# Hybrid encoder trunk on one core: SSD decay masks on GpSimd, fp32 state products, and split weights kept in DRAM

## Chip, cores and metric

The kernel runs on 1 core of one Trainium2 chip. The metric is the device time of one execution in microseconds (us), lower is better. The median of runs stands for a kernel.

## The reference, cut

One layer of a trunk over 2048 frames of a new stream (the prompt) and 8 running streams of 16 frames (the sample), all fp32, model width 1024:

```python
h = W_out [ gMLP heads (u * (W_s v + b)) || Mamba-2 SSD heads ] (x W_in)
x = LayerNorm(ALPHA * x + h)
x = LayerNorm(ALPHA * x + relu(x W1)^2 W2)
```

The part that the change touches is the SSD scan in the mixer, by chunks of 128 positions, 16 heads of 64 in two groups that share B and C:

```python
acum = cumsum(dt * a)                                  # within a chunk
decay = exp(where(causal, acum[i] - acum[j], -inf))
cb = einsum('bcign,bcjgn->bcijg', C, B)
y_diag = einsum('bcijg,bcijgr,bcjgr,bcjgrp->bcigrp', cb, decay, dt, x)
st = einsum('bcjgn,bcjgr,bcjgrp->bcgrpn', B, exp(acum[-1] - acum) * dt, x)
# over chunks: h = exp(acum[-1]) * h + st
y_off = einsum('bcign,bcgrpn,bcigr->bcigrp', C, h_start, exp(acum))
```

and the projection `x W_in` (1024 x 4624) ahead of it, whose weights the change keeps in another form.

## The kernel before

The 2176 rows are 17 chunks of 128; chunk 0 holds the sample. The mixer (`mixer_heads`) goes over three blocks of 6, 6 and 5 chunks. In each block it goes over 18 units, each a tile of 256 columns of `W_in`, in the order z0, x4, x5, x0, x1, z1, x2, x3, z2, z3, u0 to u3, v0 to v3. A unit multiplies the block's rows by its weights in a split form: each fp32 operand becomes a high and a low part of the type float32r (`split`: a cast on ScalarE at L55 gives the high part, a subtraction on VectorE at L56 the low part), and three products (high high, high low, low high; `PASSES`) are added up in PSUM. Units x and u run as `fl_matmul` (L217, 384 or 256 moving columns), units z and v as `tl_matmul` (L225, 256 columns). For every unit of every block, `load_w` reads the weights in two halves of 512 KB into a staging pool of three buffers and splits them into one of two buffers `w`.

Results of the units go through DRAM. After z1 and after z3 the tasks `ssd(b, j, g)` of the block's chunks j for the two groups g are put in a list, after v3 the tasks `gmlp`; `run(1)` emits one task behind each unit, so a block's last tasks run under the next block's units, and the last ones under the output projection. The program is then put in order by the compiler's scheduler, so that a task's instructions stand between the matmuls of the units. Each engine runs its own list in order. All loads and stores are issued from SP, in order.

A task `ssd` loads `xs`, `bt` (B, positions on partitions), `bc` (B and C transposed), `e` (the cumulative sums `at` of 8 heads, broadcast over partitions, 512 KB) and `z`. TensorE forms `pc` = C B^T (L419); VectorE multiplies it by the triangle `tri` into `cbm` (L421). For 4 of 8 heads (`NACT`) ScalarE forms the clipped difference of cumulative sums with Relu (L425), for the other 4 VectorE does (L427); two exponentials of 512 columns follow (L429, L431). VectorE multiplies the 1024 columns of `e` by `cbm` (L432); TensorE takes the eight products `yd` with `xdt` (L439). The chunk's state `st` is B times `xwt`, and `yo` is C times the state before it; both are three passes over split operands (`product`, L395), for which `bt`, `xwt`, `bc` and the state are split each time (`sm`, `xw_hi`, `xw_lo`, `h_hi`, `h_lo`; the wide ones come from the pool `fp` of 8 buffers). For chunk 0 there is a loop over 8 streams instead, with a plain fp32 `yo` (L469), `st` from split operands (L471), and loads `h` of the streams' states. There are 34 tasks: 2 of chunk 0, and 32 others, of which 30 have a `yo`. VectorE and GpSimd then combine the parts, and a gated norm goes to DRAM (L504).

After the mixer come the output projection (L679) and the feed-forward network (L876, L1064), which the change leaves as they are.

Of the kernel before, what the change touches and what calls it, by code (L numbers as in the profile page):

```python
# [14 lines left out]
P = 128  # L15
# [11 lines left out]
EPS = 1e-5  # L27
BLOCKS = [(0, 6), (6, 6), (12, 5)]
PASSES = ((0, 0), (0, 1), (1, 0))
NACT = 4  # L30
KORDER = [(q, i, k) for q in range(2) for i in range(3) for k in range(4 * q, 4 * q + 4)]


# [57 lines left out]
def mixer_heads(ctx, tc, right, psA, A, O, dr, small, sp, ident, select, rsqrt, split, yg_d, ys_d):  # L91
# [15 lines left out]

    order = ["z0", "x4", "x5", "x0", "x1", "z1", "x2", "x3", "z2", "z3", "u0", "u1", "u2", "u3", "v0", "v1", "v2", "v3"]

    def load_w(u):  # L110
        w = wp.tile([P, 2, KD, 272], F32R, name="w", tag="w")
        for q in range(2):
            load_w_half(w, u, q)
        return w

    def load_w_half(w, u, q):
        n = 272 if u == "z0" else 256
# [23 lines left out]
    for j in range(1, BLOCKS[0][1]):  # L141
        for q in range(2):
            load_x_half(j, q)

    def const(name, src, shape):
        t = cl.tile(shape, F32, name=name)
# [177 lines left out]
    def decays(b):  # L324
        c0, n = BLOCKS[b]
        s = state[b]
        N = n * NH
        tmp = lambda nm: small.tile([P, 6 * NH], F32, name=nm, tag="dtmp", bufs=4)[:, :N]
        xr = s["dt"][:, :n].rearrange("p c h -> p (c h)")
        na = tmp("na")  # L330
        nc.vector.tensor_scalar(na, xr, -1.0, None, op0=ALU.mult)
        nc.vector.tensor_tensor(na, na, xr, op=ALU.min)
        u = tmp("u")
        nc.scalar.activation(u, na, AF.Exp)
        q = tmp("q")
        nc.vector.tensor_scalar(q, u, 2.0, None, op0=ALU.add)
        nc.vector.reciprocal(q, q)
        nc.vector.tensor_mul(u, u, q)
        nc.vector.tensor_mul(q, u, u)
        p = tmp("p")  # L340
        nc.vector.tensor_scalar(p, q, 2.0 / 15, 2.0 / 13, op0=ALU.mult, op1=ALU.add)
        for k in (11, 9, 7, 5, 3, 1):
            nc.vector.tensor_mul(p, p, q)
            nc.vector.tensor_scalar(p, p, 2.0 / k, None, op0=ALU.add)
        nc.vector.tensor_mul(p, p, u)
        dt = s["dt"].rearrange("p c h -> p (c h)")[:, :N]
        nc.vector.scalar_tensor_tensor(dt, xr, 0.0, p, op0=ALU.max, op1=ALU.add)
        da = s["da"]
        dav = da[:, :N]
        nc.vector.tensor_mul(da[:, :N].rearrange("p (c h) -> p c h", h=NH), s["dt"][:, :n],  # L350
                             av.unsqueeze(1).to_broadcast([P, n, NH]))
        d0 = NH if c0 == 0 else 0
        pa = psB.tile([P, 512], F32, name="pa", tag="b")
        for m, m8, o in ((tri, tri8, 0), (gt, gt8, 128), (ones, None, 256)):
            if d0 and m8 is not None:
                nc.tensor.matmul(pa[:, o:o + d0], m8, da[:, :d0], start=True, stop=True)
            lo = d0 if m8 is not None else 0
            nc.tensor.matmul(pa[:, o + lo:o + N], m, da[:, lo:N], start=True, stop=True)
        nc.vector.tensor_copy(s["acum"][:, :N], pa[:, :N])
        nc.scalar.activation(s["ea"][:, :N], pa[:, :N], AF.Exp)  # L360
        nc.scalar.activation(s["dw"][:, :N], pa[:, 128:128 + N], AF.Exp)
        nc.scalar.activation(s["bd"][:, :N], pa[:, 256:256 + N], AF.Exp)
        nc.vector.tensor_mul(s["dw"][:, :N], s["dw"][:, :N], dt)
        pt = psB.tile([P, 512], F32, name="pta", tag="b")
        nc.tensor.matmul(pt[:N, :P], da[:, :N], tri, start=True, stop=True)
        at = small.tile([P, 2, P], F32, name="at", tag="at", bufs=1)
        nc.vector.tensor_copy(at[:N, 0], pt[:N, :P])
        nc.sync.dma_start(s["at"][d0:N], at[d0:N, 0])
        if d0:
            p8 = psB.tile([P, 512], F32, name="p8", tag="b")  # L370
            nc.tensor.matmul(p8[:d0, :P], da[:, :d0], tri8, start=True, stop=True)
            nc.vector.tensor_copy(at[:d0, 1], p8[:d0, :P])
            nc.sync.dma_start(s["at"][:d0], at[:d0, 1])

            dm = small.tile([P, NS, NH], F32, name="dm", tag="dm", bufs=1)
            nc.vector.tensor_mul(dm, ind.unsqueeze(2).to_broadcast([P, NS, NH]),
                                 da[:, :NH].unsqueeze(1).to_broadcast([P, NS, NH]))
            pd = psB.tile([P, 512], F32, name="pd", tag="b")
            nc.tensor.matmul(pd[:, :P], ones, dm.rearrange("p s h -> p (s h)"), start=True, stop=True)
            bd8 = cl.tile([P, NS, NH], F32, name="bd8")  # L380
            nc.scalar.activation(bd8.rearrange("p s h -> p (s h)"), pd[:, :P], AF.Exp)
            s["bd8"] = bd8
# [7 lines left out]
        split(*t, src)  # L390
        return t

    def product(ps, a, b, start=True, stop=True):
        for i, (p, q) in enumerate(PASSES):
            nc.tensor.matmul(ps, a[p], b[q], start=start and i == 0, stop=stop and i == 2)  # L395

    heads = lambda a: a.rearrange("p (h d) -> p h d", h=8)

    def ssd(b, j, g):
# [17 lines left out]
        nc.sync.dma_start(z, s["z"][j, :, g * 512:(g + 1) * 512])  # L417
        pc = psB.tile([P, 512], F32, name="pc", tag="b")
        nc.tensor.matmul(pc[:, :P], bc[:, 0], bc[:, 1], start=True, stop=True)  # L419
        cbm = bp.tile([P, P], F32, name="cbm", tag="cbm")  # L420
        nc.vector.tensor_mul(cbm, pc[:, :P], tri8 if dec else tri)  # L421
        for h in range(8):
            i = j * NH + 8 * g + h
            if h < NACT:
                nc.scalar.activation(e[:, h], e[:, h], AF.Relu, bias=s["acum"][:, i:i + 1], scale=-1.0)  # L425
            else:
                nc.vector.tensor_scalar(e[:, h], e[:, h], s["acum"][:, i:i + 1], 0.0, op0=ALU.subtract, op1=ALU.min)  # L427
        if NACT:
            nc.scalar.activation(e[:, :NACT], e[:, :NACT], AF.Exp, scale=-1.0)  # L429
        if NACT < 8:  # L430
            nc.scalar.activation(e[:, NACT:], e[:, NACT:], AF.Exp)  # L431
        nc.vector.tensor_mul(e, e, cbm.unsqueeze(1).to_broadcast([P, 8, P]))  # L432
        xdt = bp.tile([P, 512], F32, name="xdt", tag="xd", bufs=3)
        nc.gpsimd.tensor_mul(heads(xdt), heads(xs), s["dt"][:, j, 8 * g:8 * g + 8].unsqueeze(2).to_broadcast([P, 8, HD]))
        xwt = bp.tile([P, 512], F32, name="xwt", tag="xd", bufs=3)
# [2 lines left out]
        for h in range(8):  # L438
            nc.tensor.matmul(yd[:, h * HD:(h + 1) * HD], e[:, h], xdt[:, h * HD:(h + 1) * HD], start=True, stop=True)  # L439
        yo = None  # L440
        sm = bp.tile([P, 4, P], F32R, name="sm", tag="sm", bufs=1)
        if dec:
            yo = psB.tile([P, 512], F32, name="yo", tag="b")

# [29 lines left out]
                nc.sync.dma_start(O["ssm_sample"][r][:, g * 512:(g + 1) * 512], h0)  # L474
        else:
            st = psB.tile([P, 512], F32, name="st", tag="b")
            split(sm[:, 0], sm[:, 1], bt)
            product(st, (sm[:, 0], sm[:, 1]), wide(xwt, "xw"))
            hn = bp.tile([P, 512], F32, name="hn", tag=f"hn{g}")
            if first:  # L480
                nc.vector.tensor_copy(hn, st)
            else:
                yo = psB.tile([P, 512], F32, name="yo", tag="b")
                split(sm[:, 2], sm[:, 3], bc[:, 1])
                product(yo, (sm[:, 2], sm[:, 3]), wide(hst[g], "h"))
                nc.gpsimd.tensor_mul(heads(hn), heads(hst[g]), col("bd"))
                nc.vector.tensor_add(hn, hn, st)
            hst[g] = hn
# [73 lines left out]
    for i, (b, u) in enumerate(units):  # L562
        c0, n = BLOCKS[b]
        if u == "z0":
            N = n * P
            s = state[b] = {
                "u": dr.tile([P, 8, N], F32, name=f"u{b}"), "v": dr.tile([n, P, D], F32, name=f"v{b}"),
                "z": dr.tile([n, P, D], F32, name=f"z{b}"), "xs": dr.tile([n, P, D + 256], F32, name=f"xs{b}"),
                "bc": dr.tile([P, 2, 2, N], F32, name=f"bc{b}"), "at": dr.tile([n * NH, P], F32, name=f"at{b}"),
                "dt": cl.tile([P, 6, NH], F32, name=f"dt{b}", tag="dt", bufs=2),  # L570
                "vst": cp.tile([P, 6, 4, 6], F32, name=f"vst{b}", tag="vst", bufs=2),
            }
            for k in ("da", "acum", "ea", "dw", "bd"):
                s[k] = cl.tile([P, 6 * NH], F32, name=f"{k}{b}", tag=k, bufs=1 if k == "da" else 2)
        if i + 1 < len(units):
            nxt[i + 1] = load_w(units[i + 1][1])
        w = nxt.pop(i)
        {"x": unit_x, "z": unit_z, "v": unit_v, "u": unit_u}[u[0]](b, w, int(u[1]))
        if u == "v3" and b + 1 < len(BLOCKS):
            load_x(BLOCKS[b + 1][0], range(BLOCKS[b + 1][1]))  # L580
        if u == "z0":
            decays(b)
        if (b, u) == (0, "x5"):
            gmlp_constants()
        if u == "z1":
            tasks += [(ssd, b, j, 0) for j in range(n)]
        if u == "z3":
            tasks += [(ssd, b, j, 1) for j in range(n)]
        if u == "v3":
            tasks += [(gmlp, b, j) for j in range(n)]  # L590
            if b == len(BLOCKS) - 1:
                break
        run(1)
# [556 lines left out]
```

## Time and profile before

| | us |
|---|---|
| median of 3 runs | 2850.16 |
| lowest and highest run | 2849.03, 2855.03 |
| profiled execution, its own time | 2852.59 |
| span of its trace | 2850.6 |
| TensorE busy in the span | 2759.4 |
| VectorE busy in the span | 1989.4 |
| GpSimd busy in the span | 386.9 |

The profiled execution's own time is 2.0 us over the span of its trace, which begins and ends with the program's own instructions. Busy time of TensorE has matmuls overlapped. Granted clock 1.00 is TensorE's full speed.

### The profile page before, as it was taken

What the parts mean: (1) busy time and instruction counts of PE and PEld (TensorE: products, weight loads), DVE (VectorE), ACT (ScalarE), POOL (GpSimd) and SP (SyncE); (2) the same over time, 40 slices, a digit from 0 to 9 for tenths busy, and PEclk for the clock granted to TensorE, in tenths of its full rate; (3) what the DMA queues carried; (4) which work ended last, traced back from release to release, by engine and by line L of the source; (5) the groups of instructions that cost most, each with busy time, mean ns of one, the idle gap of its engine ahead of it and who ended that gap; (6) DMA issues with size and microseconds to landing.
All of it is one profiled execution on the core that took longest, in us unless ns stands there. A gap on an engine that the chain in (4) does not pass through costs nothing.

```text
span 2850.6 us, 42737 instructions
## 1 busy us (share of the span) xinstructions
PE 2759.4 (97%) x15876; PEld 2546.1 (89%) x15876; DVE 1989.4 (70%) x3218; ACT 1202.5 (42%) x2152; POOL 386.9 (14%) x509
## 2 busy tenths in 40 slices
PE   9999999999999998999998999999999999999998
PEld 8998999999999997887878999999999888888886
DVE  6687878778788777756558777776776344544887
ACT  5445434444444442110115555555665333323343
POOL 1223313323234212100100000000000000000022
PEclk9999999999999999999999999999999999999999
DMA  5465576555565548988569999986877455545764
GB/s 195 137 199 184 183 221 189 163 163 173 186 208 168 182 150 281 286 263 276 174 199 366 317 347 367 348 303 241 284 239 234 154 175 175 177 147 182 261 212 168
DMA packets 420800, 632.49 MB, mean 222 GB/s; under 512 B 74592, under 2 KB 309488, under 8 KB 414448
## 3 DMA queue, kind: packets, MB, share of 16 engines
q1 hardware_dynamic: 420592, 629.77, 67.3%
q8 instruction: 124, 2.03, 0.3%
q14 instruction: 84, 0.69, 0.1%
HBM read 436.16 MB, written 193.51 MB: 221 GB/s over the span
## 4 chain that ended last, share of the span: by engine, by line
PE 65%; DMA 16%; DVE 12%; issue 3%; ACT 2%; POOL 1%; SPq 1%; DVEq 0%; ACTq 0%; POOLq 0%
PE pf L876 22%; PE pf L1064 21%; PE psfl L217 7%; PE pstl L225 6%; PE po L679 4%; DMA e<-at 2%; DMA w1p<-in_w_ff 2%; DMA w1s<-w1p 2%; DVE w L56 1%; PE pf L1029 1%; DVE acc L294 1%; PE yd L439 1%; DMA v<-v 1%; DMA xs<-xs 1%; DMA xv<-xsum 1%
## 5 line engine op out<-in xcount | busy, mean ns | idle before, releaser
L876 PE MATMUL pf<-xt,w 128*128 128x384 f32 (+1 forms) x4032 | 672.0, 329 | 22.0 <-ACT w L55 10.7
L876 PEld LDWEIGHTS pf<-xt,w 128*128 128x128 f32 x4032 | 668.9, 189 | 25.3 <-ACT w L55 11.5
L1064 PE MATMUL pf<-w,ht 128*128 128x512 f32 x2688 | 618.0, 389 | 0.7 <-ACT ht L55 0.7
L1064 PEld LDWEIGHTS pf<-w,ht 128*128 128x128 f32 x2688 | 504.5, 188 | 105.6 <-ACT ht L55 1.1
L217 PE MATMUL psfl<-xw,w 128*128 128x384 f32 (+1 forms) x2880 | 499.6, 331 | 0.0
L217 PEld LDWEIGHTS psfl<-xw,w 128*128 128x128 f32 x2880 | 480.8, 190 | 8.1 <-issue 5.6
L225 PE MATMUL pstl<-w,xw 128*128 128x256 f32 (+1 forms) x3264 | 400.3, 283 | 6.9 <-ACT w L55 6.9
L225 PEld LDWEIGHTS pstl<-w,xw 128*128 128x128 f32 x3264 | 395.0, 189 | 10.2 <-ACT w L55 6.9
L679 PE MATMUL po<-wout,mx 128*128 128x512 f32 x1632 | 379.4, 394 | 10.5 <-ACT mx L55 6.2
L679 PEld LDWEIGHTS po<-wout,mx 128*128 128x128 f32 x1632 | 309.2, 190 | 77.5 <-ACT mx L55 6.8
L56 DVE TENSOR_TENSOR ht<-hr,ht 128x1536 fp32r<-128x1536 f32 (+1 forms) x84 | 132.4, 1576 | 185.2 <-ACT ht L55 182.6
L55 ACT CAST ht<-hr 128x1536 fp32r<-128x1536 f32 (+1 forms) x84 | 112.3, 1337 | 216.1 <-PE pf L1064 194.5
L76 POOL TENSOR_SCALAR frs<-fmv 128x1 f32<-128x1 f32 x17 | 8.9, 525 | 1301.3 <-DVE fmv L983 1300.7
L55 ACT CAST w<-w2r 128x512 fp32r<-128x512 f32 x192 | 110.7, 618 | 135.2 <-PE pf L1064 92.2
L56 DVE TENSOR_TENSOR w<-w2r,w 128x512 fp32r<-128x512 f32 x192 | 124.5, 684 | 61.2 <-ACT w L55 60.9
L55 ACT CAST w<-w1s 128x512 fp32r<-128x512 f32 x192 | 118.6, 619 | 83.3 <-PE pf L876 77.3
L56 DVE TENSOR_TENSOR w<-ws,w 128x1024 fp32r<-128x1024 f32 (+1 forms) x108 | 148.4, 1401 | 5.2 <-ACT w L55 5.1
L56 DVE TENSOR_TENSOR w<-w1s,w 128x512 fp32r<-128x512 f32 x192 | 131.8, 688 | 22.6 <-ACT w L55 18.1
L294 DVE SCALAR_TENSOR_TENSOR acc<-raw,cw,acc 128x640 f32<-128x640 f32 (+1 forms) x108 | 104.1, 964 | 13.4 <-ACT acc L288 12.6
L55 ACT CAST w<-ws 128x1024 fp32r<-128x1024 f32 (+1 forms) x108 | 108.2, 1050 | 7.2 <-DMA ws<-in_w_in 6.0
L55 ACT CAST mx<-mxs 128x512 fp32r<-128x512 f32 x34 | 20.1, 620 | 164.8 <-DMA mxs<-yg 106.2
L56 DVE TENSOR_TENSOR w<-w1r,w 128x512 fp32r<-128x512 f32 x96 | 66.0, 688 | 33.1 <-ACT w L55 31.1
(227 smaller groups left out, 3135.7 us busy)
## 6 DMA issues: line engine op xcount, KB each, us to landing
ws<-in_w_in SPq DMA_DIRECT2D x102, 512.0 KB, 5.2
w1s<-w1s SPq DMA_DIRECT2D x48, 1024.0 KB, 7.6
hr<-hv SPq DMA_DIRECT2D x56, 768.0 KB, 5.3
w1r<-in_w_ff SPq DMA_DIRECT2D x48, 512.0 KB, 7.8
hv<-hs SPq DMA_DIRECT2D x32, 768.0 KB, 5.9
w2r<-w2s SPq DMA_DIRECT2D x80, 256.0 KB, 4.3
e<-at SPq DMA_DIRECT2D x34, 512.0 KB, 6.9
x<-x SPq DMA_DIRECT2D x33, 512.0 KB, 5.7
```

The lines of the kernel that those rows point to most:

```text
L55: nc.scalar.copy(hi, src)
L56: nc.vector.tensor_sub(lo, src, hi.bitcast(F32))
L76: nc.gpsimd.tensor_scalar(out, var, scale, eps, op0=ALU.mult, op1=ALU.add)
L217: nc.tensor.matmul(ps[:, :n], w[:, a, k, f * P:(f + 1) * P], xw[:, b, k, o:o + n], start=(q, i, k) == KORDER[0], stop=(q, i, k) == KORDER[-1])
L225: nc.tensor.matmul(ps[:, :n], xw[:, a, k, j * P:(j + 1) * P], w[:, b, k, :n], start=(q, i, k) == KORDER[0], stop=(q, i, k) == KORDER[-1])
L294: nc.vector.scalar_tensor_tensor(aa, raw[:, k:k + npr], cw[:, ft, k:k + 1], aa, op0=ALU.mult, op1=ALU.add)
L439: nc.tensor.matmul(yd[:, h * HD:(h + 1) * HD], e[:, h], xdt[:, h * HD:(h + 1) * HD], start=True, stop=True)
L679: nc.tensor.matmul(acc[c][d], m[c][k // 4][:, a, k % 4], W[q][:, w, i, d * 512:(d + 1) * 512], start=k == 0 and (a, w) == (0, 0), stop=k = ...
L876: nc.tensor.matmul(o, W[i][:, u, k], X[i][:, v, k, :n], start=q + k == 0 and not more, stop=q == 2 and k == 3, skip_group_check=True)
L1029: nc.tensor.matmul(ps[d], h[:, u, k, f], w[d][:, v], start=k + f + q == 0, stop=(k, f, q) == (n - 1, 1, 2))
L1064: nc.tensor.matmul(acc[l], h[:, u, m, j * P:(j + 1) * P], w[m][:, v], start=kg + q + m == 0, stop=(kg, q, m) == (3, 2, 3))
```

## The change

Four things change, all inside the mixer.

- **Decays.** `cbm` and the clipped differences go. GpSimd writes -1e30 over the entries of `e` above the diagonal (`select`, an affine select over 128x1024; for chunk 0 two more to keep streams apart). ScalarE takes the exponential of each head's 128 columns with the negated cumulative sum as bias (8 instructions). VectorE multiplies `e` by `pc` straight from PSUM.
- **State products.** `st` and `yo` of chunks 1 to 16 are one plain fp32 matmul each, on `bt`, `xwt`, `bc` and the state as they are. Their splits go. Chunk 0 keeps its own.
- **Weight parts.** In block 0 each unit's split weights `w` are written to DRAM, 2 MB (`keep_parts`). In blocks 1 and 2 `load_w` reads these 2 MB straight into `w`; the loads of the raw halves and the splits go.
- `acum` is stored negated (`nacum`).

```diff
+    def load_w(b, u):
+
         w = wp.tile([P, 2, KD, 272], F32R, name="w", tag="w")
+        n = 272 if u == "z0" else 256
+        if b > 0:
+            nc.sync.dma_start(w[:, :, :, :n].bitcast(F32), parts[u])
+            return w
         for q in range(2):
             load_w_half(w, u, q)
+        keep_parts(u, w)
         return w
+
+    def keep_parts(u, w):
+        n = 272 if u == "z0" else 256
+        parts[u] = dr.tile([P, 2, KD, n], F32, name=f"w_{u}")
+        nc.sync.dma_start(parts[u], w[:, :, :, :n].bitcast(F32))
...
-        nc.vector.tensor_copy(s["acum"][:, :N], pa[:, :N])
+        nc.vector.tensor_scalar(s["nacum"][:, :N], pa[:, :N], -1.0, None, op0=ALU.mult)
...
-        cbm = bp.tile([P, P], F32, name="cbm", tag="cbm")
-        nc.vector.tensor_mul(cbm, pc[:, :P], tri8 if dec else tri)
+
+        select(e, [[0, 8], [1, P]], 0, -1, fill=NEVER)
+        if dec:
+            e4 = e.rearrange("p h (s t) -> p h s t", s=NS)
+            select(e4, [[0, 8], [-DS, NS], [0, DS]], 0, 1, fill=NEVER)
+            select(e4, [[0, 8], [DS, NS], [0, DS]], DS - 1, -1, fill=NEVER)
         for h in range(8):
             i = j * NH + 8 * g + h
-            if h < NACT:
-                nc.scalar.activation(e[:, h], e[:, h], AF.Relu, bias=s["acum"][:, i:i + 1], scale=-1.0)
-            else:
-                nc.vector.tensor_scalar(e[:, h], e[:, h], s["acum"][:, i:i + 1], 0.0, op0=ALU.subtract, op1=ALU.min)
-        if NACT:
-            nc.scalar.activation(e[:, :NACT], e[:, :NACT], AF.Exp, scale=-1.0)
-        if NACT < 8:
-            nc.scalar.activation(e[:, NACT:], e[:, NACT:], AF.Exp)
-        nc.vector.tensor_mul(e, e, cbm.unsqueeze(1).to_broadcast([P, 8, P]))
+            nc.scalar.activation(e[:, h], e[:, h], AF.Exp, bias=s["nacum"][:, i:i + 1])
+        nc.vector.tensor_mul(e, e, pc[:, :P].unsqueeze(1).to_broadcast([P, 8, P]))
...
-            split(sm[:, 0], sm[:, 1], bt)
-            product(st, (sm[:, 0], sm[:, 1]), wide(xwt, "xw"))
+            nc.tensor.matmul(st, bt, xwt, start=True, stop=True)
...
-                split(sm[:, 2], sm[:, 3], bc[:, 1])
-                product(yo, (sm[:, 2], sm[:, 3]), wide(hst[g], "h"))
+                nc.tensor.matmul(yo, bc[:, 1], hst[g], start=True, stop=True)
```

## Rows read from the trace of the kernel before

**Rows 1.** The page, part 1: busy us (share of the span) xinstructions.

```profile
PE 2759.4 (97%) x15876; PEld 2546.1 (89%) x15876; DVE 1989.4 (70%) x3218; ACT 1202.5 (42%) x2152; POOL 386.9 (14%) x509
```

**Rows 2.** Windows: busy us (x) of PE, PEld, DVE, ACT, POOL; clock, DMA share, GB/s.

```profile
0.00:387.00 387.00, 371.35 (x2468) 355.09 (x2469) 298.14 (x543) 189.74 (x394) 98.80 (x182) 1.00 0.58 182
387.00:598.00 211.00, 199.62 (x1357) 196.15 (x1357) 163.67 (x279) 88.44 (x179) 62.73 (x73) 0.98 0.60 182
598.00:761.00 163.00, 162.92 (x1162) 160.65 (x1161) 132.87 (x243) 80.52 (x182) 48.29 (x49) 1.00 0.53 170
...
870.00:1021.00 151.00, 144.42 (x983) 140.06 (x982) 114.57 (x199) 72.64 (x168) 56.19 (x55) 0.94 0.57 177
...
1085.00:1140.00 55.00, 44.40 (x207) 35.30 (x206) 42.78 (x80) 15.89 (x22) 16.28 (x16) 0.94 0.98 317
```

**Rows 3.** Waits of PE, 387:1085: who <- by whom: total us, times, longest.

```profile
PE yd L439 <- DVE e L432: 10.6, 6, 3.6
PE sg L533 <- DVE v L522: 6.4, 2, 3.5
```

**Rows 4.** Waits of PE, 0:387.

```profile
PE yo L469 <- DMA h<-in_state_ssm: 4.1, 3, 2.0
```

**Rows 5.** The chain that ended last, 0:600: start us, us, what.

```profile
100.14 16.92 PE pstl L225 x144
...
290.39 0.86 PE yo L469 x2
...
585.32 0.70 PE yo L395 x3
```

**Rows 6.** Timeline, 944:953: start us, us, instruction, idle before it.

```profile
946.99 1.42 DVE L56 TENSOR_TENSOR h_lo<-hn,h_hi 128x512 fp32r<-128x512 f32 x1
947.82 1.49 POOL L436 TENSOR_TENSOR xwt<-xs,dw 128x512 f32<-128x512 f32 x1
...
948.67 1.73 DVE L432 TENSOR_TENSOR e<-e,cbm 128x1024 f32<-128x1024 f32 x1
...
950.54 2.80 PE L439 MATMUL yd<-xdt,e 128*128 128x64 f32 x16 [3.00 <-DVE e L432]
```

**Rows 7.** Groups by line, whole span: busy us, mean ns of one, idle before.

```profile
L56 DVE TENSOR_TENSOR w<-ws,w 128x1024 fp32r<-128x1024 f32 x102 | 140.4, 1403 | 4.0 <-ACT w L55 3.9
...
L425 ACT ACTIVATE e<-e,acum 128x128 f32<-128x128 f32 x136 | 43.9, 391 | 72.1 <-DMA e<-at 72.0
...
L427 DVE TENSOR_SCALAR e<-e,acum 128x128 f32<-128x128 f32 x136 | 37.6, 333 | 33.9 <-DMA e<-at 33.7
...
L56 DVE TENSOR_TENSOR xw_lo<-xwt,xw_hi 128x512 fp32r<-128x512 f32 x34 | 30.6, 899 | 38.3 <-ACT xw_hi L55 38.2
...
L56 DVE TENSOR_TENSOR h_lo<-hn,h_hi 128x512 fp32r<-128x512 f32 x30 | 22.8, 759 | 0.0
...
L421 DVE TENSOR_TENSOR cbm<-pc,tri 128x128 f32<-128x128 f32 x34 | 9.6, 281 | 6.2 <-PE pc L419 6.1
```

**Rows 8.** Groups by line of POOL, whole span.

```profile
L69 POOL TENSOR_SCALAR_AFFINE_SELECT wt<-wt 128x1024 f32<-128x1024 f32 x1 | 1.1, 1091 | 12.3 <-DMA wt<-in_gmlp_wsT 12.3
```

**Rows 9.** DMA issues, whole span: KB each, median us to landing.

```profile
ws<-in_w_in SPq DMA_DIRECT2D x102, 512.0 KB, 5.2
w1s<-w1s SPq DMA_DIRECT2D x48, 1024.0 KB, 7.6
...
e<-at SPq DMA_DIRECT2D x34, 512.0 KB, 6.9
```

**Rows 10.** Waits of the DMA queue of SP, 0:1060.

```profile
SPq L504 <- DVE xs L503: 104.5, 21, 10.0
...
SPq L415 <- PE yd L439: 10.3, 9, 3.7
```

**Rows 11.** Timeline of SP, 970:990.

```profile
972.64 0.42 SPq L415 DMA_DIRECT2D e<-at  x1
```

**Rows 12.** Timeline of DVE, 1003.5:1008.

```profile
1006.14 1.22 DVE L432 TENSOR_TENSOR e<-e,cbm 128x1024 f32<-128x1024 f32 x1
```

More of the change, by code (lines that the diff above doesn't have):

```diff
@@ L29 @@
 PASSES = ((0, 0), (0, 1), (1, 0))
-NACT = 4
+NEVER = -1e30
 KORDER = [(q, i, k) for q in range(2) for i in range(3) for k in range(4 * q, 4 * q + 4)]
@@ L108, in mixer_heads @@
     order = ["z0", "x4", "x5", "x0", "x1", "z1", "x2", "x3", "z2", "z3", "u0", "u1", "u2", "u3", "v0", "v1", "v2", "v3"]
-    def load_w(u):
+    parts = {}
+    def load_w(b, u):
         w = wp.tile([P, 2, KD, 272], F32R, name="w", tag="w")
+        n = 272 if u == "z0" else 256
+        if b > 0:
+            nc.sync.dma_start(w[:, :, :, :n].bitcast(F32), parts[u])
+            return w
         for q in range(2):
             load_w_half(w, u, q)
+        keep_parts(u, w)
         return w
+    def keep_parts(u, w):
+        n = 272 if u == "z0" else 256
+        parts[u] = dr.tile([P, 2, KD, n], F32, name=f"w_{u}")
+        nc.sync.dma_start(parts[u], w[:, :, :, :n].bitcast(F32))
     def load_w_half(w, u, q):
@@ L143, in mixer_heads @@
             load_x_half(j, q)
+    keep_parts("z0", w0)
     def const(name, src, shape):
@@ L391, in wide @@
         return t
-    def product(ps, a, b, start=True, stop=True):
-        for i, (p, q) in enumerate(PASSES):
-            nc.tensor.matmul(ps, a[p], b[q], start=start and i == 0, stop=stop and i == 2)
     heads = lambda a: a.rearrange("p (h d) -> p h d", h=8)
@@ L440, in ssd @@
         yo = None
-        sm = bp.tile([P, 4, P], F32R, name="sm", tag="sm", bufs=1)
         if dec:
@@ L572, in mixer_heads @@
             }
-            for k in ("da", "acum", "ea", "dw", "bd"):
+            for k in ("da", "nacum", "ea", "dw", "bd"):
                 s[k] = cl.tile([P, 6 * NH], F32, name=f"{k}{b}", tag=k, bufs=1 if k == "da" else 2)
         if i + 1 < len(units):
-            nxt[i + 1] = load_w(units[i + 1][1])
+            nxt[i + 1] = load_w(*units[i + 1])
         w = nxt.pop(i)
```

## The prediction

> **What bounds the kernel now.** I read the page first: TensorE is busy for 97% of the span and no other engine comes near it [rows 1]. The windows over the mixer say the same stage by stage, and they say more: in 598:761 TensorE is busy for 162.92 of 163 us at a granted clock of 1.00, although VectorE has 132.87 us of work there, 82% [rows 2]. A full VectorE alone holds nothing up. Around this stretch TensorE loses a little: 199.62 of 211 us at clock 0.98, and 144.42 of 151 us at clock 0.94 [rows 2]. So the mixer can give back only TensorE's waits and the time at half clock (1.2 instead of 2.4 GHz) that follows some of them.
>
> The waits of TensorE from 387 to 1085, blocks 1 and 2, come next. Most belong to `yd`, which waits for VectorE's product `e`: 10.6 us in 6 waits; `sg` of the gMLP task waits 6.4 us for VectorE [rows 3]. In block 0 the largest wait inside the stream is for the loads of the sample's states, 4.1 us [rows 4]. The clock adds (1 - 0.98) x 211 = 4.2 and (1 - 0.94) x 151 = 9.1, together 13.3 us of full-speed time lost [rows 2]. What the change can win is of the order of 10.6 + 6.4 + 13.3 = 30 us, about 1% of the time.
>
> The timeline of the longest wait in 870:1021 shows its make-up. `yd` stood idle for 3.00 us for L432; before L432 VectorE did `h_lo` in 1.42 us, and L432 itself took 1.73 us while GpSimd ran `xwt` for 1.49 us [rows 6]. The same L432 takes 1.22 us elsewhere [rows 12], and `h_lo` has a mean of 0.759 us [rows 7].
>
> **The change part by part.** *State products.* Three float32r passes over 512 columns take 0.70 us in the chain, one fp32 product of 512 columns (two records) 0.86 us [rows 5]. That is 0.16 us more for each of 32 `st` and 30 `yo`: 62 x 0.16 = +9.9 us on the engine that sets the end. Nothing hides it. The Trainium skill says so too (FP8 and Floating Point Precision, TensorE Precision Notes): true fp32 goes through the array four times. By that rule the price would be 0.70 x 4/3 - 0.70 = 0.23 us each, +14.5 us in all, an estimate from that page; the trace's 0.86 lies below it and is what I use.
>
> *Splits that go.* A task loses `xw_lo` 0.899, `h_lo` 0.759, `cbm` 0.281 and four differences of 0.333, 3.3 us of VectorE, and two small splits besides [rows 7]. Each of the 36 units of blocks 1 and 2 loses two splits of 1.403 us [rows 7], 36 x 2.8 = 101 us of VectorE. None of this is on TensorE's path by itself (598:761, above). It counts only where such an instruction stands between `pc` and `yd`. In the wait of 3.00 us, `h_lo` (1.42) and `cbm` (0.28) go, and L432 may fall back from 1.73 to 1.22: 2.2 us of 3.0. Other waits have gelu or conv work in that place, which stays. I take 6 of the 10.6 us, with 0 and 10.6 as bounds; of `sg`, whose VectorE queue is shorter too, 1 of 6.4 (bounds 0 and 6.4). Of the clock's 13.3 us I take 8, in the same proportion (bounds 0 and 13.3): -6 - 1 - 8 = -15 us.
>
> *Decays.* The select over 1024 columns has one row before, 1.091 us on GpSimd [rows 8]; 34 + 4 of them are 41 us on an engine with 48.29 of 163 us busy [rows 2]. Then 8 exponentials at 0.391 us, 3.1 us on ScalarE, in place of 4 x 0.391 and two wider ones [rows 7]. The path from the landing of `e` to L432 gets longer by the select and by some 1 us. It has room: an `e` load follows the `yd` of two tasks before (two buffers; SP waits for `yd` there [rows 10]), so the load issued at 972.64 [rows 11] is the one multiplied at 1006.14 [rows 12], 33 us later, of which the landing takes 6.9 [rows 9]. Price 0, and if the cover were gone 1.1 + 1 us in each of 34 tasks, +70 us. Reading `pc` from PSUM in L432 shows in no row; bounds 1.22 and 1.73, I take 1.22, since one operand from SBUF goes.
>
> *Weight parts.* Blocks 1 and 2 read 2 MB in place of 1 MB for each of 36 units. The load can start only when TensorE has left the `w` two units back, and must land within one unit. 512 KB land in 5.2 us, 1024 KB in 7.6 [rows 9]; with 2.4 us for each further 512 KB an estimate is 12.4 us for 2 MB. Bounds: 2.1 MB at 182 GB/s / 0.58 = 314 GB/s [rows 2] is 6.7 us, and twice the 7.6 is 15.2. A unit of 144 matmuls takes 16.92 us [rows 5], one of five chunks 120/144 of it, 14.1, and one with an SSD task under it has that task's matmuls besides. So 12.4 us fit, price 0, with 1.7 us to spare in block 2's bare units. In block 0, 18 writes of 2.1 MB add 38 MB; at 314 GB/s that is 120 us of all DMA engines in 387, and the share goes from 0.58 to 0.89. The raw loads there are staged well ahead. The streams' states are not: their wait of 4.1 us may grow by half, +2 us (bounds 0 and one write, 6.7 us, in each of 3 waits, 20).
>
> Sum: +9.9 - 15 + 2 = -3 to -4 us. The profiled execution took 2852.6, which would become 2849; it stands 2.4 us above the median of the runs, against which the forecast is 2846.
>
> **The rivals.** *The waits go altogether* (0.14). VectorE falls so far that every `yd` finds its `e`: -10.6 - 6.4 - 13.3 + 9.9 = -20 us, 2830. For it speaks that all six waits end on VectorE; against it, that 598:761 has none at 82%, so load is not what makes them.
>
> *The waits stay* (0.15). They are a matter of where the order puts `pc` and `yd`, not of VectorE's load; then fp32 is paid and little returned, +10 + 2 - 3: 2859. It decides if fewer than half of the six waits shrink. This is the case in which the change does not do what it could.
>
> *Weights land late* (0.10), slower. SP issues in order, and its store L504 waits 104.5 us in 21 times, 5 us each [rows 10]. If the load of `w` stands behind one, 12.4 + 5 = 17.4 us exceeds a unit of 14.1. In block 2 some six units have no SSD task under them (the first ones and the last two): 6 x 3.3 = 20 us, 2866. It decides once landing plus SP's delay is over the unit's time.
>
> *Block 0's writes* (0.08), slower: all of the bound of 20 us, 2863.
>
> *GpSimd holds VectorE* (0.08): 41 us of selects beside VectorE's two-operand work lengthen it as the 1.73 against 1.22 shows, which puts about 5 us of `yd` waits back: 2851. The Trainium skill has the rule (SBUF — State Buffer, SBUF: two separate sides): VectorE with two SBUF inputs and GpSimd exclude each other for a whole instruction. The trace agrees with it in the 1.73 us. It would also free L432, whose second input is then in PSUM.
>
> **How the numbers follow.** The forecast has 0.45 and its own range 2836 to 2853; 0.27 of it lies below 2844.5 and 0.18 above. A time within 0.2% (5.7 us) of 2850.2 is about what cannot be told from no change. Faster: 0.27 + 0.14 = 0.41. Within 0.2%: 0.18, 0.06 of GpSimd and 0.04 of the waits that stay, 0.28. Slower: the rest of these two, 0.11 + 0.02, and 0.18, is 0.31. Leaving out the far half of the fastest case and of the two late ones, the range is 2829 to 2867.
>
> **What would show it.** `st` and `yo` as two records of 0.86 us a pair, 62 pairs. `yd` waits for L432 of about 4 to 5 us in all in blocks 1 and 2, and a clock nearer 1 in the stretch that was at 0.94. No wait of psfl or pstl for a DMA into `w`. In block 0 a DMA share near 0.9 with the wait for the states below 7 us. Wrong if psfl or pstl wait for `w`, if `yd` waits for GpSimd or ScalarE instead, or if block 0 alone grows by over 10 us.

## The result, and the profile after

The changed kernel takes 2838.59 us (median), the kernel before 2852.86 us in the runs beside it: a ratio of 0.9944, 95% interval 0.9924 to 0.9964, faster by 14.3 us between the medians and 16 us by the ratio. The forecast was 4 us faster.

The engines on the page of the changed kernel, as in [rows 1]:

```profile
PE 2755.8 (97%) x15814; PEld 2525.9 (89%) x15814; DVE 1811.7 (64%) x2852; ACT 1097.7 (39%) x2024; POOL 395.0 (14%) x547
```

TensorE has lost 4 us of busy time, VectorE 178, ScalarE 105. The windows of the changed kernel, columns as in [rows 2]:

```profile
0.00:387.00 387.00, 371.15 (x2438) 349.87 (x2439) 259.41 (x438) 175.26 (x377) 108.98 (x196) 1.00 0.87 281
387.00:598.00 211.00, 208.07 (x1410) 203.24 (x1410) 129.86 (x223) 66.51 (x157) 68.76 (x82) 0.98 0.78 246
598.00:761.00 163.00, 163.00 (x1136) 155.35 (x1136) 95.74 (x174) 58.03 (x148) 46.90 (x57) 1.00 0.65 216
...
870.00:1021.00 151.00, 148.81 (x1065) 140.63 (x1064) 88.50 (x133) 52.78 (x150) 52.46 (x64) 1.00 0.71 230
```

Read the clock and the first two figures. The stretches are cut at the same times in both kernels, so the later ones do not hold quite the same work: block 2 begins at 756.5 in place of 761.4. From 870 to 1021 the clock stood at 0.94 and is now at 1.00, and TensorE is busy for 148.81 us in place of 144.42; from 387 to 598 it is 208.07 in place of 199.62. VectorE's work there fell from 114.57 to 88.50 and from 163.67 to 129.86. Block 0 pays in DMA: a share of 0.87 where it was 0.58. The waits of TensorE in blocks 1 and 2 of the changed kernel, against [rows 3], and then its wait for the streams' states in block 0, against [rows 4]:

```profile
PE pa L372 <- DVE da L364: 3.6, 2, 2.7
PE yd L446 <- DVE e L439: 2.2, 2, 1.7
PE sg L537 <- DVE v L526: 1.0, 1, 1.0
```

```profile
PE yo L475 <- DMA h<-in_state_ssm: 5.7, 3, 2.2
```

`yd` now waits 2.2 us for VectorE in place of 10.6, `sg` 1.0 in place of 6.4. The largest is `pa`, at the start of a block, 3.6 in place of 2.1.

The last matmul of the units z and v begins 20.0 us earlier. The line's instructions in the changed kernel and, below, in the kernel before (count, shortest, median, longest in ns, first and last start):

```profile
L239 PE MATMUL pstl<-w,xw x3264: 274/280/1201, 6.6 to 1064.9; 128*128 128x256 f32 x167, 128*128 128x272 f32 x25
```

```profile
L225 PE MATMUL pstl<-w,xw x3264: 274/280/683, 6.9 to 1084.9; 128*128 128x256 f32 x167, 128*128 128x272 f32 x25
```

By the count of the units' matmuls, block 0 takes 1.4 us longer than before (block 1 begins at 388.6 in place of 387.2), and blocks 1 and 2 take 676.3 us in place of 697.7, which is 21.4 us less. From the last unit to the end it is 2836.5 - 1064.9 = 1771.6 us, where it was 2850.6 - 1084.9 = 1765.7. So 5.9 us of the 20 do not arrive.

The price of fp32 is plain in the chain that ended last, 560 to 700 of the changed kernel (start us, us, what). It holds TensorE and nothing else there:

```profile
599.82 12.03 PE psfl L231 x69
611.85 0.22 PE pc L429 x2
612.07 4.70 PE psfl L231 x27
616.77 1.73 PE yd L446 x16
618.50 0.91 PE st L483 x2
619.41 0.86 PE yo L489 x2
```

`st` takes 0.91 us and `yo` 0.86. A period of one unit with its task, from one `pc` to the next, is 20.43 us (611.85 to 632.28), where the same chain of the kernel before has 20.13 (598.61 to 618.74).

The groups of the new decays, and the DMA issues that matter:

```profile
L438 ACT ACTIVATE e<-e,nacum 128x128 f32<-128x128 f32 x272 | 83.6, 389 | 71.9 <-POOL e L69 71.9
...
L69 POOL TENSOR_SCALAR_AFFINE_SELECT e<-e 128x1024 f32<-128x1024 f32 x38 | 46.2, 1217 | 97.9 <-DMA e<-at 91.9 <-DVE xs L502 4.3 <-DMA yg<-ug 1.6
...
L439 DVE TENSOR_TENSOR e<-e,pc 128x1024 f32<-128x1024 f32 x34 | 41.2, 1213 | 21.9 <-PE pc L429 21.9
```

```profile
w<-w_x SPq DMA_DIRECT2D x12, 2048.0 KB, 10.4
...
ws<-in_w_in SPq DMA_DIRECT2D x34, 512.0 KB, 7.5
e<-at SPq DMA_DIRECT2D x34, 512.0 KB, 7.0
...
w_x<-w SPq DMA_DIRECT2D x6, 2048.0 KB, 9.7
```

The select takes 1.217 us where one row before said 1.091 [rows 8], a head's exponential 0.389. A load of 2 MB into `w` lands in 10.4 us (9.1 to 9.9 for the units u, v and z). TensorE waits for no such load in the mixer.

### The profile page after: what moved, and what is told of

Same layout as the page of the kernel before. It is cut to its first block, busy times and chain, and to the rows that moved or that the text cites. A ratio compares the mean times of both kernels' runs of the same rounds, so it can differ in the third digit from the quotient of the medians.

```text
span 2836.5 us, 42155 instructions
## 1 busy us (share of the span) xinstructions
PE 2755.8 (97%) x15814; PEld 2525.9 (89%) x15814; DVE 1811.7 (64%) x2852; ACT 1097.7 (39%) x2024; POOL 395.0 (14%) x547
## 4 chain that ended last, share of the span: by engine, by line
PE 76%; DMA 12%; DVE 7%; SPq 1%; issue 1%; ACT 1%; POOL 1%; ACTq 0%; DVEq 0%; POOLq 0%
PE pf L880 22%; PE pf L1068 21%; PE psfl L231 12%; PE pstl L239 10%; PE po L683 4%; PE yd L446 2%; DMA w1s<-w1p 2%; DMA w1p<-in_w_ff 2%; PE pf L1033 2%; DMA xv<-xtt 1%; PE sg L537 1%; PE st L483 1%; DMA e<-at 1%; DMA v<-vo 1%; PE yo L489 1%
## 5 line engine op out<-in xcount | busy, mean ns | idle before, releaser
L880 PE MATMUL pf<-xt,w 128*128 128x384 f32 (+1 forms) x4032 | 672.9, 329 | 24.7 <-ACT w L55 13.6
L239 PE MATMUL pstl<-w,xw 128*128 128x256 f32 (+1 forms) x3264 | 410.2, 286 | 8.5 <-ACT w L55 6.6
L683 PEld LDWEIGHTS po<-wout,mx 128*128 128x128 f32 x1632 | 308.2, 190 | 81.4 <-ACT mx L55 10.7
L308 DVE SCALAR_TENSOR_TENSOR acc<-raw,cw,acc 128x640 f32<-128x640 f32 (+1 forms) x108 | 114.0, 1055 | 18.3 <-ACT acc L302 16.9
L438 ACT ACTIVATE e<-e,nacum 128x128 f32<-128x128 f32 x272 | 83.6, 389 | 71.9 <-POOL e L69 71.9
L247 ACT ACTIVATE gt<-gt 128x256 f32<-128x256 f32 (+1 forms) x116 | 52.3, 451 | 95.2 <-DVE gt L246 95.2
L871 ACT ACTIVATE hc<-hc 128x384 f32<-128x384 f32 (+3 forms) x144 | 87.1, 608 | 2.0
## 6 DMA issues: line engine op xcount, KB each, us to landing
w<-w_x SPq DMA_DIRECT2D x12, 2048.0 KB, 10.4
```

Source lines behind the costliest of these rows:

```text
L239: nc.tensor.matmul(ps[:, :n], xw[:, a, k, j * P:(j + 1) * P], w[:, b, k, :n], start=(q, i, k) == KORDER[0], stop=(q, i, k) == KORDER[-1])
L308: nc.vector.scalar_tensor_tensor(aa, raw[:, k:k + npr], cw[:, ft, k:k + 1], aa, op0=ALU.mult, op1=ALU.add)
L438: nc.scalar.activation(e[:, h], e[:, h], AF.Exp, bias=s["nacum"][:, i:i + 1])
L683: nc.tensor.matmul(acc[c][d], m[c][k // 4][:, a, k % 4], W[q][:, w, i, d * 512:(d + 1) * 512], start=k == 0 and (a, w) == (0, 0), stop=k = ...
L871: nc.scalar.activation(t, t, AF.Square)
L880: nc.tensor.matmul(o, W[i][:, u, k], X[i][:, v, k, :n], start=q + k == 0 and not more, stop=q == 2 and k == 3, skip_group_check=True)
```

## The experiments

Each ratio is to runs of the kernel before on the same chip. In the expectations, theory A is the prediction's: only what stands on VectorE between `pc` and `yd` makes the waits. Rival B says that the load as a whole does.

**The parts alone.** Three kernels each make one part of the change in the kernel before: the stored weights (W), the fp32 products (P), the decays (D).

```diff
 # parts_only
+        if b > 0:
+            nc.sync.dma_start(w[:, :, :, :n].bitcast(F32), parts[u])
+            return w
...
 # fp32_only
-            product(st, (sm[:, 0], sm[:, 1]), wide(xwt, "xw"))
+            nc.tensor.matmul(st, bt, xwt, start=True, stop=True)
...
 # decay_only
+        select(e, [[0, 8], [1, P]], 0, -1, fill=NEVER)
...
-        nc.vector.tensor_mul(e, e, cbm.unsqueeze(1).to_broadcast([P, 8, P]))
+        nc.vector.tensor_mul(e, e, pc[:, :P].unsqueeze(1).to_broadcast([P, 8, P]))
```

> The kernel before with one part of the change, the split weights kept in DRAM. Theory A (what stands on VectorE between pc and yd makes the waits, and the splits of the state stand there, the splits of the weights rarely do): within 4 us of before, the yd waits in blocks 1 and 2 still 7 us or more of 10.6. Rival B (VectorE's and ScalarE's load as a whole makes the waits, and 101 us of weight splits are the largest piece of it): 10 to 25 us faster, yd waits under 4 us. Rival C (the writes in block 0 crowd the DMA engines): block 0 alone ends 5 us or more later.

> The kernel before with one part of the change, plain fp32 state products without their splits. Theory A: +10 us of TensorE time for 62 products, and 10 to 14 us back since the state's splits no longer stand between pc and yd: 0 to 4 us faster, yd waits under 5 us. Rival B (load as a whole): the 10 us are paid and less than half of the waits goes: 5 to 10 us slower.

> The kernel before with one part of the change, the masks on GpSimd and all exponentials on ScalarE. Theory A: one VectorE step of 0.28 us less between pc and yd, 0 to 4 us faster. Rival B (load as a whole): 1.6 us less VectorE work per task, 2 to 6 us faster. Rival D (GpSimd's selects hold VectorE or come late in its queue): 3 us or more slower, with yd waiting for L432 or ScalarE.

**The parts in pairs.** The changed kernel with one part taken back gives the other three corners.

```diff
 # no_fp32
-            nc.tensor.matmul(st, bt, xwt, start=True, stop=True)
+            product(st, (sm[:, 0], sm[:, 1]), wide(xwt, "xw"))
...
 # no_decay
-        select(e, [[0, 8], [1, P]], 0, -1, fill=NEVER)
+        nc.vector.tensor_mul(cbm, pc[:, :P], tri8 if dec else tri)
...
 # no_parts
-            nxt[i + 1] = load_w(*units[i + 1])
+            nxt[i + 1] = load_w(units[i + 1][1])
```

> The changed kernel with the state products as three passes over split operands again. Theory A: the 10 us of fp32 come back, but the splits stand between pc and yd again and bring the waits back: 0 to 6 us from the changed kernel. Rival B (load): with the weights' splits gone VectorE has room for the state's splits, so the 10 us are won: about 10 us faster than the changed kernel, 24 us faster than before.

> The changed kernel with the decays of before (triangle product, differences on ScalarE and VectorE). If the parts add up as they were measured alone, the decays cost about 4 us and this is 3 to 5 us faster than the changed kernel, 0.9925 to 0.9935 of before. Rival: once the weight splits are gone the masks on GpSimd do help, since VectorE loses 1.6 us per task; then 2 to 5 us slower than the changed kernel, 0.995 to 0.997 of before.

> The changed kernel with the weights loaded raw and split in every block again. Rival B (load): this keeps the paid fp32 and no room on VectorE in the units, 3 to 10 us slower than before, yd waits of 8 us or more. Theory A (only what stands between pc and yd counts): both products' splits and cbm are gone from there, so yd waits under 4 us and 0 to 6 us faster than before.

All eight corners. The columns behind the ratio are counted from one profile of each, in us: when block 1 begins, by the count of the units' matmuls; the length of blocks 1 and 2; and what that length is made of. "Idle" is the time in which TensorE runs nothing, "half clock" is half of the time that it works at a granted clock of 0.5 (1.2 GHz), and "work" is the rest, its work at full speed (2.4 GHz). The last column is the mean of the 22 tasks in these blocks from the start of `pc` to the end of VectorE's product with `e`, the gap of theory A.

| parts | ratio to before, 95% | block 1 begins | blocks 1 and 2 | work | idle | half clock | gap |
|---|---|---|---|---|---|---|---|
| none | 1 | 387.2 | 697.7 | 661.4 | 23.0 | 13.4 | 4.50 |
| W | 0.9963 (0.9948 to 0.9977) | 389.0 | 684.5 | 663.2 | 16.2 | 5.1 | 4.42 |
| P | 1.0010 (0.9997 to 1.0023) | 387.6 | 700.3 | 667.8 | 21.4 | 11.1 | 3.74 |
| D | 1.0014 (1.0001 to 1.0026) | 386.5 | 702.5 | 662.1 | 26.8 | 13.6 | 3.97 |
| W P | 0.9994 (0.9977 to 1.0011) | 400.0 | 681.1 | 666.7 | 9.3 | 5.1 | 3.23 |
| W D | 0.9973 (0.9961 to 0.9986) | 390.2 | 678.6 | 662.0 | 11.6 | 5.0 | 3.27 |
| P D | 0.9981 (0.9960 to 1.0002) | 389.4 | 691.7 | 667.9 | 15.3 | 8.5 | 3.29 |
| W P D | 0.9944 (0.9924 to 0.9964) | 388.6 | 676.3 | 666.3 | 7.0 | 3.0 | 2.62 |

The stored weights help in each of the four pairs of rows that differ in them alone: by 0.37, 0.16, 0.41 and 0.37% of the time, and by 13 to 24 us in blocks 1 and 2. There they take 14 to 24 us off idle and half clock together, and leave the work within 2 us. P adds 3.5 to 6.4 us of work. The other two parts gain nothing alone. Beside each other they help: P with D by 0.33% without W and by 0.29% with it, D with P by 0.29 and 0.50%. Neither theory expected that. The waits of `yd` in blocks 1 and 2 of parts_only, fp32_only and decay_only, in this order:

```profile
PE yd L453 <- DVE e L446: 6.0, 6, 2.2
```

```profile
PE yd L435 <- DVE e L428: 9.9, 5, 2.9
```

```profile
PE yd L435 <- DVE e L428: 11.5, 9, 2.6
```

Theory A fails as the whole account. It had parts_only within 4 us of before, and fp32_only and decay_only 0 to 4 us faster; by the ratios they are 11 us faster, 3 us slower and 4 us slower. fp32_only takes `h_lo` and `xw_lo` out from between `pc` and `yd`, and `yd` still waits 9.9 us. parts_only leaves them there, and the wait falls to 6.0 us. These two waits alone would not decide it, since another order of the same work moves the wait by 4.5 us (below). The gap decides more: W alone leaves it as it was (4.50 and 4.42 us), and takes 15 us off idle and half clock; P alone shortens it by 0.76 us, and takes 4 us off. In the kernel before, splits of the weights fill only 1.5 us of all 22 gaps. Rival B does not hold as it stands either: it expected no_fp32 to be about 10 us faster than the changed kernel and no_parts 3 to 10 us slower than before, and they are 8 us slower and 5 us faster. Nor did either expectation of no_decay, 0.9925 to 0.9935 or 0.995 to 0.997, come true. Rival C, a block 0 longer by 5 us or more in parts_only, did not come either: it is 1.8 us. The window of parts_only, to be read against 144.42 and 0.94 in [rows 2], shows what else came back, the clock:

```profile
870.00:1021.00 151.00, 145.52 (x1025) 141.49 (x1025) 107.90 (x204) 64.51 (x165) 44.12 (x55) 0.98 0.73 235
```

D helps beside W and P by 0.50%, but hardly in blocks 1 and 2: of the 15.0 us between the two profiles 4.7 lie there and 11.4 in block 0, which in no_decay lasts until 400.0. From 200 to 300 the clock of no_decay is 0.95, and below it the changed kernel has 0.99:

```profile
200.00:300.00 100.00, 92.11 (x502) 84.20 (x502) 63.96 (x106) 43.38 (x92) 33.69 (x37) 0.95 0.75 245
```

```profile
200.00:300.00 100.00, 95.31 (x541) 87.43 (x540) 58.28 (x85) 48.25 (x109) 38.97 (x49) 0.99 0.82 267
```

Over its block 0 the half clock costs no_decay 9.8 us (1.7 in the changed kernel), and idle time is 19.2 us (15.9). What brought this about was not tried. In no_decay VectorE also waits for the landing of `e` itself, as the differences are its work again:

```profile
DVE e L437 <- DMA e<-at: 58.5, 27, 6.1
```

In the kernel before, the same view has 33.7 us in 19 waits for these differences. The masks give this wait to GpSimd. But only 12.9 of the 58.5 us fall before 400, so this wait does not explain the loss in block 0.

**A second write in block 0.**

```diff
+        again = dr.tile([P, 2, KD, n], F32, name=f"w2_{u}")
+        nc.sync.dma_start(again, w[:, :, :, :n].bitcast(F32))
```

> The changed kernel with the split weights of block 0 written a second time to a tensor that nothing reads, 38 MB more. If the writes cost TensorE time by crowding the DMA engines, the price of a second write bounds that of the first: block 1 begins 8 us or more later. If the queue has room and only the streams' states are late, 0 to 4 us later.

The ratio is 1.0219 (1.0190 to 1.0249), 79 us slower than the changed kernel's. Its windows:

```profile
0.00:387.00 387.00, 349.69 (x2324) 340.46 (x2325) 225.42 (x380) 154.55 (x311) 67.08 (x132) 0.96 1.03 346
387.00:598.00 211.00, 177.13 (x989) 158.23 (x989) 136.74 (x222) 62.84 (x152) 94.99 (x112) 0.86 0.70 229
```

With 38 MB more the DMA engines are full from 0 to 387, at 346 GB/s. Block 1's matmuls begin at 376.3, earlier than in the changed kernel, where both expectations had them later; but only 5 of block 0's 12 tasks have had their product with `e` by then (all 12 in the changed kernel), and blocks 1 and 2 take 770.2 us, with the clock at 0.86 from 387 to 598. So the first write left no room for a second of its size, and is nearly free only because there was room for one. A second write also holds each `w` and the queue of SP for longer; this run does not tell that from the full engines.

**VectorE's and ScalarE's load put back.** Two kernels give VectorE back a load like that of the splits, the first on `w`, the second on constants. A third gives ScalarE copies.

```diff
 # vector_back, after the load of w in blocks 1 and 2, for each half
+                nc.vector.tensor_sub(s[:, :, :n], w[:, 0, k, :n].bitcast(F32), w[:, 1, k, :n].bitcast(F32))
...
 # vector_free
+                nc.vector.tensor_sub(scratch, tri.unsqueeze(1).to_broadcast([P, 8, P]), ones.unsqueeze(1).to_broadcast([P, 8, P]))
...
 # scalar_free
+                nc.scalar.copy(scratch, tri.unsqueeze(1).to_broadcast([P, 8, P]))
```

> The changed kernel with two subtractions of 128x1024 on VectorE put back for each unit of blocks 1 and 2, into staging buffers that nothing reads: VectorE's load as with splits, ScalarE's casts and the raw loads still gone. If VectorE's time made the waits, 8 to 14 us of the gain go and yd waits come back to 5 us or more. If it was ScalarE's casts or the chain load, cast, subtract that held things up, 0 to 3 us slower than the changed kernel.

> The changed kernel with two subtractions of 128x1024 on VectorE added for each unit of blocks 1 and 2, on constants, into a scratch tile that nothing reads, so that unlike the version before they wait for no load: some 90 to 100 us of VectorE time alone. If VectorE's time made the waits, 6 to 14 us of the gain go and yd waits in blocks 1 and 2 come back to 5 us or more. If it was ScalarE's casts or the chain load, cast, subtract, 0 to 3 us slower than the changed kernel.

> The changed kernel with two copies of 128x1024 on ScalarE added for each unit of blocks 1 and 2, from a constant into a scratch tile: some 75 us of ScalarE time alone. If VectorE is what mattered, 0 to 3 us slower than the changed kernel. If ScalarE's casts held up the exponentials and the evictions of PSUM, 5 us or more of the gain go.

vector_back has a ratio of 1.0077 (1.0049 to 1.0104), more than the whole gain lost. But it tells nothing of load alone, since VectorE, in order, now waits for each load of `w`. Its waits from 387 to 1085:

```profile
DVE ws L121 <- DMA w<-w_x: 34.5, 10, 13.2
DVE ws L121 <- DMA w<-w_u: 32.5, 8, 5.5
DVE ws L121 <- DMA w<-w_v: 22.7, 8, 5.0
```

vector_free has 1.0073 (1.0054 to 1.0093), and fails as a test too. As its instructions wait for nothing, the scheduler ran them in block 0. The windows show VectorE busy for 312.34 us there (259.41 in the changed kernel), and in 870:1021 it has 86.02, no more than the 88.50 of the changed kernel (all 72 subtractions start before 191 us):

```profile
0.00:387.00 387.00, 346.38 (x2140) 324.57 (x2140) 312.34 (x451) 157.49 (x332) 138.85 (x169) 0.95 0.77 251
...
870.00:1021.00 151.00, 146.39 (x1028) 138.36 (x1028) 86.02 (x129) 47.01 (x126) 50.98 (x62) 0.98 0.75 237
```

All it shows is what 92 us of work among the splits of block 0 cost: block 1 begins at 435.0 in place of 388.6, and blocks 1 and 2 take 680.1 us. scalar_free has 0.9907 (0.9891 to 0.9924). Its copies went into block 0 as well, where ScalarE has room; that it beats the changed kernel is not a merit of useless work, and the next pair bears on it.

**Another order.** The scheduler writes the order anew for each program. Two kernels add only one tiny instruction per unit.

```diff
-        w = nxt.pop(i)
+        w = nxt.pop(i); nc.vector.memset(spare, 0.0)
```

> The kernel before with one clearing of a 128x1 tile on VectorE added per unit, some 5 us of VectorE time in all, which makes the scheduler put the program in another order. If the order alone moves little, within 3 us of before. If it moves as much as the parts differ, 4 us or more either way.

> The changed kernel with the same clearing of a 128x1 tile per unit. If the order alone moves little, within 3 us of the changed kernel, 0.9934 to 0.9955 of before. If the changed kernel owes part of its gain to a lucky order, 4 us or more slower.

noise_before has 1.0000 (0.9990 to 1.0011), noise_after 0.9932 (0.9907 to 0.9956). In the profiles, blocks 1 and 2 take 704.3 us in place of 697.7, and 669.6 in place of 676.3. Their work stays (661.8 and 665.9 us); idle and half clock together go from 36.4 to 42.5 and from 10.0 to 3.7. The waits of `yd` in noise_before, against 10.6 in [rows 3]:

```profile
PE yd L439 <- DVE e L432: 15.1, 8, 3.3
```

The gap hardly moves (4.47 for 4.50 and 2.68 for 2.62). So the order alone moves these two blocks by some 7 us either way in single profiles. Differences of that size between the corners of the table, those of P and D among them, are not safely the parts' own, and nor is the 11.4 us in block 0 of no_decay, which comes from one order. The 13 to 24 us of W are larger, and have one sign in all four pairs.

## Why the prediction was right in its sign and short in its size

The forecast of 2846 was 7 us too long; the measured 2838.6 lies about midway between it and the rival in which the waits go altogether, 2830. The two profiles close the sum. Their spans differ by 14.2 us: +6.0 us for TensorE's work in the mixer (1.1 in block 0, 4.9 in blocks 1 and 2), -26.3 for idle time (15.9) and half clock (10.4) in blocks 1 and 2, +0.3 for block 0's idle time, and +5.9 after the mixer. The prediction had +9.9, -15, +2 and 0.

- **State products, +9.9 us: right in kind, somewhat high.** By the chain, 0.91 + 0.86 against the 0.75 and 0.70 us that three passes took in most tasks is 0.32 us per task of the two, and the period grew by 0.30; 62 products at 0.16 are the 9.9 us of the prediction. Counted over whole blocks the work grew by 6.0 us, a count that moves by up to 2 us with parts other than P. The sum by the rule of four passes, from the Trainium skill (FP8 and Floating Point Precision, TensorE Precision Notes), was 14.5 us in the prediction; the measurement decides for less.
- **Splits that go, -15 us: the step that failed.** The prediction said that a split counts only where it stands between `pc` and `yd`, since the stretch 598:761 has no waits at 82% of VectorE. By that rule the weights' 101 us of splits, which fill 1.5 us of the gaps, were worth next to nothing, and the state's splits were the gain. The runs show the reverse: W alone leaves the gap at 4.42 us and takes 15 us off idle and half clock, and P alone takes 4 off and adds 6 us of work. The stretch 598:761 is a bad witness, as its periods are long, 20 us, while block 2's are about 18 where nothing waits. The terms were short too: of `yd` 8.4 of 10.6 us went (6 expected), of `sg` 5.4 of 6.4 (1 expected), and of the clock 0.06 x 151 = 9.1 us in the second stretch, while 0.02 x 211 = 4.2 stayed in the first (8 of 13.3 expected; the proportion it names, 6 of 10.6, gives 7.5). The gap did get shorter, over block 2's ten tasks from 5.57 to 3.55 us, as the prediction had it; but P and D do that, not W (5.18), and beside W the two bring 11 us of idle and half clock for 3 us of work. One `yd` wait that is left, in the timeline of the changed kernel:

```profile
896.90 1.18 DVE L439 TENSOR_TENSOR e<-e,pc 128x1024 f32<-128x1024 f32 x1
...
898.23 1.97 PE L446 MATMUL yd<-xdt,e 128*128 128x64 f32 x16 [1.67 <-DVE e L439]
```

  The product is the 1.18 us ahead of `yd`; conv work stood before it, as the prediction said it would.
- **Decays, price 0: borne out.** The +4 us when alone (1.0014) is no more than another order does. The cover held: the product with `e` waits for `pc` alone (21.9 us, above), never for an exponential or a select, and at 1.21 us it takes the 1.22 that was assumed for `pc` from PSUM.
- **Weights land late: did not come.** 10.4 us was estimated as 12.4.
- **Block 0, +2 us beside 2.9 of fp32 (18 of the 62 products): near.** The wait for the states went from 4.1 to 5.7 us, and the block took 1.4 us longer in all. The rival of 20 us did not come, but in write_twice, with twice the writes, the kernel is 79 us slower.
- **GpSimd holds VectorE: not by the products with `e`.** The changed kernel's product, and below it that of the kernel before:

```profile
L439 DVE TENSOR_TENSOR e<-e,pc x34: 1178/1214/1224, 116.3 to 1019.4; 128x1024 f32<-128x1024 f32 x34
```

```profile
L432 DVE TENSOR_TENSOR e<-e,cbm x34: 1187/1217/2062, 117.9 to 1042.5; 128x1024 f32<-128x1024 f32 x34
```

  The longest went from 2062 to 1224 ns. It holds across the runs: in the five kernels with both operands in SBUF 16 of 170 such products take more than 1250 ns, and in the nine with one in PSUM none of 306 takes more than 1224. The Trainium skill (SBUF — State Buffer, SBUF: two separate sides) would have it so: there a VectorE instruction with two inputs in SBUF locks the pair of ports that it shares with GpSimd, and with `pc` in PSUM the product has only one. This is the side of the rule that the prediction named and did not price.
- **Not foreseen: 5.9 us lost after the mixer.** It is not the price of ending early: noise_after ends its units at 1057.0 and needs 1766.5 us from there, fp32_only ends at 1087.9 and needs 1769.3. Over all but the two kernels that put load back on VectorE it is 1766 to 1773 us, and the kernel before lies at the short end of that. The work there is the same (1700.7 and 1701.0 us), and idle time rises from 52.6 to 57.8: TensorE waits 9.7 us for ScalarE's casts of `mx` in place of 6.2, and 13.6 in place of 10.7 for those of `w` at the start of the feed-forward network. Why is left open.
- **Left open:** how W takes the waits away: whether by VectorE's time, ScalarE's casts, or the wait that each split has for its cast. Neither kernel that put VectorE's load back kept it where the splits had been.

## What to carry to other kernels

Work taken from an engine that is 70 to 80% busy can pay on the one that is full, and not only where it stands right in front of a result that the full one waits for: here most came from a part that left that gap as it was. So do not price a change by one gap, nor by a stage that happens to have slack; split the full engine's time into work, idle time and lower clock, for each part alone and beside the others. Bytes for instructions was a good trade here while the DMA engines had room, and a second portion of the same size told that there was no room for it. Where a scheduler orders the program, time a neutral edit as well, and trust a part's effect only where it is larger or holds in every combination.

## What the runs showed of the hardware

- The DMA engines moved 281 GB/s at a share of 0.87 with TensorE's idle time in block 0 at 15.9 us (15.6 at a share of 0.58), and 346 GB/s at full share with the kernel 79 us slower. What lies between the two was not run.
- VectorE's product of 128x1024 with a broadcast operand from PSUM took 1178 to 1224 ns in all 34 cases, and no more in the 306 of nine kernels; with both operands in SBUF 1187 to 2062 ns, and over 1250 ns in 16 of 170 of five kernels.
- After a wait of 1.67 us for `yd` at 898 the clock stayed at 1.00 (2.4 GHz) in the stretch 870:1021. In the kernel before, TensorE was busy up to 947.5, waited 3.00 us for `yd`, and the granted clock was 0.50 (1.2 GHz) from 951.5 to 958.3.
